# A third buffer for raw weights in the first of two layers, paid for with smaller pools of statistics

## The chip, the cores and the metric

The kernel runs on one core of a Trainium2 chip. The metric is the device time of one execution in microseconds (us). In the profile PE is TensorE's matrix multiplies, PEld its weight loads, DVE is VectorE, ACT is ScalarE, POOL is GpSimd, and SP is the queue from which this kernel issues all of its DMAs.

## What is computed

A decoder trunk of two layers on 512 positions of width 1024, in float32. The core of the reference:

```python
def even_layer(x, ...):               # layer 0
    q, k, v, g_ret, xb, g_lru = split(x @ w_in)          # six parts of 1024 columns
    ret = retention(rope(q), rope(k) * dk**-0.5, v)      # 8 heads, decay per head
    ret = groupnorm(ret) * gn_g + gn_b
    ret = ret * silu(g_ret)
    lru = rg_lru_branch(xb, ...) * silu(g_lru)           # conv of width 4, gates, scan
    return concat([ret, lru]) @ w_out

def odd_layer(x, ...):                # layer 1
    q, k, v, g = split(x @ w_in)                         # four parts of 2048 columns
    out = diff_attention(rope(q) * dh**-0.5, rope(k), v, lam)   # 8 heads, two softmax maps each
    out = rmsnorm(out) * subln_g * (1 - lambda_init) * silu(g)
    return out @ w_out

h = layer_norm(alpha * h + layer(h))  # after each layer
```

## The kernel before

**Number format.** Matrix products are made from float32 in two parts. `split` (L140) writes a high part with ACT (a cast, L146) and a low part with DVE (a subtraction, L147). `mm3` (L149) then issues three matmuls: high by high (L150) and the two cross products (L151, L152). Each weight passes through this as well.

**Weights.** There are 144 weight tiles of 128 x 1024 (512 KB each), named w0, w1 and so on in the order of their use. Tiles w0 to w63 belong to the first layer. `fetch` (L164) takes the next one. It allocates a raw tile from the pool `wraw` (two buffers), issues its DMA from SP (L172), and splits it into a pair from the pool `wsp` (five pairs). In the profile `w_r` is a raw tile, `w19h` and `w19l` are the parts of weight 19. A raw buffer is free again when its cast and its subtraction are done. A pair is free when the last matmul with that weight is done. `take` (L179) calls `fetch` until the weight in use and up to two more have been written into the program.

**Order.** PE and SP run in the order in which the program is written (`manual_schedule`, L118). ACT, DVE and POOL are ordered by the framework when the kernel is built, by priorities (`high_priority`) and by when it reckons an instruction to be ready. On the chip each engine runs its own queue in order and waits on semaphores.

**The first layer** runs a list of units, `ev` (L249): products of one weight with the whole input (`t_unit`: gates `gl` and `gr`, `xb`, `q`, `k`), value projections `v` in two halves of four weights (`s_unit`), and output products (`out_unit`). Between the matmuls of a unit `side.tick()` (L190) lets the heads' own work in: `retention` (L432) and `lru` (L475) are generators that are resumed after set numbers of ticks. `retention` makes four score products (`rs`), multiplies them with a decay table on DVE (`rsd`, L440), splits them (`r`), sums them with the values (`ro`), squares and averages the result (`rq`, `rv`), and normalizes it. `lru` makes a convolution (`xc`), two gates (`pr`, `pi`) and a scan. Both use the pool `es` of temporaries. The decay tables (`dec`, two buffers in the pool `two`) and the parameters of the first layer norm (`ln`) are also loaded from SP (L156). The pools `es`, `qkp` and `two` belong to the first layer and close with it (`phase`, L368 and L589).

**Statistics.** The pool `small` has four buffers a tag. In it are the means of the value projection (`vm`, L418), the two halves' sums of a layer norm (`bst`), their mean and variance (`bmv`), the reciprocal deviation (`lrs`) and, in one block of the last norm, `lnm`. A layer norm handles four blocks of 128 positions.

Of the kernel before, what the change touches and what calls it, by code (L numbers as in the profile page):

```python
# [8 lines left out]
F32 = mybir.dt.float32  # L9
# [5 lines left out]
P = 128  # L15
D = 1024
# [80 lines left out]
def trunk(ctx: ExitStack, tc: tile.TileContext, a):  # L97
# [3 lines left out]
    def pool(name, bufs, stack=ctx, **kw):  # L101
        return stack.enter_context(tc.tile_pool(name=name, bufs=bufs, **kw))

    const = pool("const", 1)
    big = pool("big", 1)
    wraw = pool("wraw", 2)
    wsp = pool("wsp", 5)
    vp = pool("vp", 4)
    mixp = pool("mixp", 3)
# [3 lines left out]
    small = pool("small", 4)  # L113
# [8 lines left out]
    def work(name):  # L122
        return wk.tile([P, S], F32, tag="wk", name=name)
# [4 lines left out]
    def bank(pl, tag, name):  # L128
        return pl.tile([P, 512], F32, tag=tag, name=name)

    def pair(pl, shape, tag, name, **kw):
        return tuple(pl.tile(shape, F32R, tag=tag + x, name=name + x, **kw) for x in "hl")
# [4 lines left out]
    def cut(t, *ix):  # L137
        return t[0][ix], t[1][ix]

    def split(src, dst, scale=None):  # L140
        if scale is not None:
            s = sg[:, scale:scale + 1]
            nc.scalar.activation(out=dst[0], in_=src, func=AF.Identity, scale=s)
            nc.vector.scalar_tensor_tensor(out=dst[1], in0=src, scalar=s, in1=dst[0].bitcast(F32), op0=ALU.mult, op1=ALU.subtract)
            return
        nc.scalar.copy(out=dst[0], in_=src)  # L146
        nc.vector.tensor_tensor(out=dst[1], in0=src, in1=dst[0].bitcast(F32), op=ALU.subtract)  # L147

    def mm3(out, l, r, start, stop):  # L149
        nc.tensor.matmul(out=out, lhsT=l[0], rhs=r[0], start=start, stop=False)  # L150
        nc.tensor.matmul(out=out, lhsT=l[0], rhs=r[1], start=False, stop=False)  # L151
        nc.tensor.matmul(out=out, lhsT=l[1], rhs=r[0], start=False, stop=stop)  # L152

    def load(name, shape, src, pl=None, tag=None, bufs=None):
        t = (pl or const).tile(shape, F32, tag=tag or name, name=name, bufs=bufs)
        nc.sync.dma_start(out=t, in_=src)  # L156
        return t
# [6 lines left out]
    def fetch(parts=((0, D),)):  # L164
        if len(ready) < len(order):
            n = len(ready)
            src, scale = order[n]
            raw = wraw.tile([P, D], F32, tag="raw", name=f"w{n}_r")
            w = pair(extra.pop(n, wsp), [P, D], "w", f"w{n}")
            for lo, hi in parts:  # L170
                c = slice(lo, hi)
                nc.sync.dma_start(out=raw[:, c], in_=src[:, c])  # L172
                split(raw[:, c], cut(w, ALL, c), scale=scale)
                yield
            ready.append(w)
# [3 lines left out]
    def take(ahead):  # L179
        taken[0] += 1  # L180
        while len(ready) < min(taken[0] + ahead, len(order)):
            list(fetch())
        return ready[taken[0] - 1]
# [36 lines left out]
    def out_unit(mix, y, name, first, before=None, after=None, late=0):  # L220
        n = len(mix)
        w = [take(1 if n == 2 else 0) for _ in range(n)]
        for sb in range(SB):
            pss = [bank(ps_pj, "pj", f"{name}_ps{sb}{hf}") for hf in range(2)]
            steps = [(c, hf) for c in range(0, n, 2) for hf in range(2)]
            if late and sb == SB - 1:
                steps.sort(key=lambda t: t[1])
            for c, hf in steps:
                if before is not None and hf == 0:
                    before(c // 2, sb)  # L230
                for i in range(c, c + 2):
                    mm3(pss[hf], cut(mix[i], ALL, slice(sb * P, sb * P + P)), cut(w[i], ALL, slice(hf * HALF, hf * HALF + HALF)), i == 0, i == n - 1)
                    side.tick()
            for hf, ps in enumerate(pss):
                yy = y[:, sb, hf * HALF:hf * HALF + HALF]
                with tc.high_priority(late):
                    if first:
                        nc.vector.scalar_tensor_tensor(out=yy, in0=yy, scalar=ALPHA, in1=ps, op0=ALU.mult, op1=ALU.add)
                    else:
                        nc.vector.tensor_tensor(out=yy, in0=ps, in1=yy, op=ALU.add)  # L240
                    if late:
                        if hf == 0:
                            st = small.tile([P, 2, 6], F32, tag="bst", name="bst")
                        nc.vector.bn_stats(out=st[:, hf], in_=yy)
                        stats[sb] = st
            if after is not None:
                after(sb)
# [9 lines left out]
    for kind, i in ev:  # L257
        if kind in ("ro", "lo", "out"):
            order += [(eo[2 * i + j + n], None) for n in {"ro": (0,), "lo": (8,), "out": (8, 0)}[kind] for j in range(2)]
        else:  # L260
            n = 4 if kind == "v" else 1
# [67 lines left out]
    def layer_norm(y, sb, gb, late=None):  # L329
        hv = [y[:, sb, hf * HALF:hf * HALF + HALF] for hf in range(2)]  # L330
        st = stats.pop(sb, None)
        if st is None:
            st = small.tile([P, 2, 6], F32, tag="bst", name="bst")
            for hf in range(2):
                nc.vector.bn_stats(out=st[:, hf], in_=hv[hf])
        mv = small.tile([P, 2], F32, tag="bmv", name="bmv")
        nc.vector.bn_aggr(out=mv, in_=st)  # L337
        rs = small.tile([P, 1], F32, tag="lrs", name="lrs")
        if late is not None:
            ve = small.tile([P, 1], F32, tag="rs", name="lve")  # L340
            nc.vector.tensor_scalar(out=ve, in0=mv[:, 1:2], scalar1=EPS, scalar2=None, op0=ALU.add)
            nc.gpsimd.tensor_tensor(out=rs, in0=ve, in1=nhalf[:, :1], op=ALU.pow)
        else:
            rsqrt(mv[:, 1:2], rs, 1.0, EPS)
        if late:

            nm = small.tile([P, 1], F32, tag="lnm", name="lnm")
            nc.gpsimd.tensor_scalar(out=nm, in0=mv[:, 0:1], scalar1=rs, scalar2=-1.0, op0=ALU.mult, op1=ALU.mult)
            nc.scalar.activation(out=hv[1], in_=hv[1], func=AF.Identity, scale=rs, bias=nm)
            nc.gpsimd.tensor_tensor(out=hv[1], in0=hv[1], in1=gb[0][1], op=ALU.mult)  # L350
            nc.gpsimd.tensor_tensor(out=hv[1], in0=hv[1], in1=gb[1][1], op=ALU.add)
            nc.vector.scalar_tensor_tensor(out=hv[0], in0=hv[0], scalar=mv[:, 0:1], in1=gb[0][0], op0=ALU.subtract, op1=ALU.mult)
            nc.vector.scalar_tensor_tensor(out=hv[0], in0=hv[0], scalar=rs, in1=gb[1][0], op0=ALU.mult, op1=ALU.add)
            yield from enumerate(hv)
            return
        for hf in range(2):
            nc.vector.scalar_tensor_tensor(out=hv[hf], in0=hv[hf], scalar=mv[:, 0:1], in1=gb[0][hf], op0=ALU.subtract, op1=ALU.mult)
        for hf in range(2):
            nc.vector.scalar_tensor_tensor(out=hv[hf], in0=hv[hf], scalar=rs, in1=gb[1][hf], op0=ALU.mult, op1=ALU.add)
            yield hf, hv[hf]  # L360
# [7 lines left out]
    phase = ctx.enter_context(ExitStack())  # L368
    es = pool("es", 10, phase)
    qkp = pool("qkp", 2, phase)  # L370
    two = pool("two", 2, phase)
    y = big.tile([P, SB, D], F32, tag="y", name="y")
    vecs = load("vecs", [P, 8, KT], a["vecs"])
    conv_w = lambda i, c: vecs[:, i, c:c + 1]
# [37 lines left out]
    def v_even(i):  # L412
        out = []

        def evac(sb, ps):
            with tc.high_priority(P_VALUE):
                p3 = ps.rearrange("p (h e) -> p h e", e=P)
                m = small.tile([P, 4], F32, tag="vm", name="vm")  # L418
                nc.vector.tensor_reduce(out=m, in_=p3, axis=AX.X, op=ALU.add)
                nc.vector.tensor_scalar(out=m, in0=m, scalar1=1.0 / P, scalar2=None, op0=ALU.mult)  # L420
                c = work("vc")
                nc.vector.tensor_tensor(out=c.rearrange("p (h e) -> p h e", e=P), in0=p3, in1=m.unsqueeze(2).broadcast_to([P, 4, P]), op=ALU.subtract)
                t = pair(vp, [P, S], "v", f"ev{i}{sb}")
                split(c, t)
            out.append(t)

        s_unit(x, f"ev{i}", i == 1, evac, lambda sb: None)
        return out
# [89 lines left out]
    m, job, seen = {}, {}, set()  # L518
# [15 lines left out]
    for kind, i in ev:  # L534
# [5 lines left out]
        elif kind == "xb":  # L540
            if i % 2 == 0:
                raw = load(f"gw{i}", [P, 4 * P], a["gw"][i // 2], pl=es, tag="es")
# [44 lines left out]


    phase.close()  # L589
    lq = load("lq", [P, 4, P], a["lq"].partition_broadcast(P), pl=wk, tag="wk")  # L590
    nc.vector.tensor_tensor(out=lq[:, 0:2], in0=lq[:, 0:2], in1=lq[:, 2:4], op=ALU.mult)
    ls = const.tile([P, 2], F32, tag="ls", name="ls")
# [199 lines left out]
```

## Time and profile before

| | |
|---|---|
| median of three runs | 940.38 us (940.04 to 940.52) |
| the profiled execution | 940.23 us, of which 938.4 us from the first to the last instruction |
| PE busy | 922.6 us, 98% |
| PEld busy | 764.8 us, 82% |
| DVE busy | 693.8 us, 74% |
| ACT busy | 462.8 us, 49% |
| POOL busy | 59.2 us, 6% |
| granted TensorE clock, mean | 0.998 |
| DMA | 88.94 MB, mean 95 GB/s |
| loads of first-layer weights | 63 of 512 KB and one in two halves |

Two things help in reading the rows. Matmuls overlap, and the end of a matmul is modelled. Its row is longer than the distance to the next one, so lost time is seen in the starts. And a wait at the end of a row, `[1.57 <-DMA w_r<-in_ev_w]`, is idle time of that engine before the instruction, with what ended it.

### The profile page before, as it was taken

What the parts mean: (1) busy time and instruction counts of PE and PEld (TensorE: products, weight loads), DVE (VectorE), ACT (ScalarE), POOL (GpSimd) and SP (SyncE); (2) the same over time, 40 slices, a digit from 0 to 9 for tenths busy, and PEclk for the clock granted to TensorE, in tenths of its full rate; (3) what the DMA queues carried; (4) which work ended last, traced back from release to release, by engine and by line L of the source; (5) the groups of instructions that cost most, each with busy time, mean ns of one, the idle gap of its engine ahead of it and who ended that gap; (6) DMA issues with size and microseconds to landing.
All of it is one profiled execution on the core that took longest, in us unless ns stands there. A gap on an engine that the chain in (4) does not pass through costs nothing.

```text
span 938.4 us, 11555 instructions
## 1 busy us (share of the span) xinstructions
PE 922.6 (98%) x4327; PEld 764.8 (82%) x4327; DVE 693.8 (74%) x1171; ACT 462.8 (49%) x750; POOL 59.2 (6%) x118
## 2 busy tenths in 40 slices
PE   9999999999999999999999999999999999999996
PEld 7888888878888788888887888888888888888885
DVE  5877997867869988994489864578754488637677
ACT  5567786566384776423334455233453234444230
POOL 0000000000000000000001210100100101101023
PEclk9999999999999999999999999999999999999999
DMA  6562221512414123304222222132222141223102
GB/s 225 168 222 71 79 80 56 169 57 70 144 34 168 57 90 115 124 23 168 90 91 68 68 83 76 45 126 98 68 68 90 45 135 68 69 89 113 67 23 90
DMA packets 27417, 88.94 MB, mean 95 GB/s; under 512 B 3425, under 2 KB 3553, under 8 KB 27361
## 3 DMA queue, kind: packets, MB, share of 16 engines
q1 hardware_dynamic: 27360, 88.20, 28.3%
q8 instruction: 34, 0.56, 0.3%
q14 instruction: 23, 0.18, 0.1%
HBM read 86.09 MB, written 2.10 MB: 94 GB/s over the span
## 4 chain that ended last, share of the span: by engine, by line
PE 68%; DVE 16%; ACT 7%; issue 3%; DMA 3%; POOL 2%; SPq 0%; DVEq 0%; POOLq 0%; ACTq 0%
PE ov_ps L152 3%; PE ov_ps L151 3%; PE ov_ps L150 3%; PE og_ps L150 3%; PE og_ps L151 3%; PE og_ps L152 3%; PE oo_ps L150 3%; PE oo_ps L151 2%; PE oo_ps L152 2%; DMA w_r<-in_ev_w 2%; PE xb_ps L151 1%; PE xb_ps L150 1%; PE out_ps L150 1%; PE xb_ps L152 1%; PE out_ps L152 1%
## 5 line engine op out<-in xcount | busy, mean ns | idle before, releaser
L611 ACT ACTIVATE e<-as,nm 128x128 f32<-128x128 f32 (+3 forms) x64 | 33.1, 523 | 26.5 <-DVE nm L608 26.3
L642 DVE SCALAR_TENSOR_TENSOR o<-po,ars,og 128x256 f32<-128x256 f32 x32 | 15.5, 484 | 36.0 <-POOL ars L327 36.0
L608 DVE CUSTOM_DVE_ANT_0 as<-as,mask 128x128 f32<-128x128 f32 (+3 forms) x64 | 30.3, 510 | 1.9 <-PE as L152 1.9
L618 POOL TENSOR_SCALAR zr<-z 128x1 f32<-128x1 f32 x32 | 11.2, 351 | 316.3 <-ACT e L611 316.3
L326 POOL TENSOR_SCALAR rs_t<-bmv 128x1 f32<-128x1 f32 x6 | 2.2, 375 | 419.7 <-DVE bmv L337 419.7
L638 ACT ACTIVATE po<-po 128x256 f32<-128x256 f32 x32 | 11.9, 372 | 25.2 <-PE po L152 25.0
L326 POOL TENSOR_SCALAR rs_t<-ss,zr 128x1 f32<-128x1 f32 x32 | 16.0, 502 | 129.2 <-ACT po L638 123.8
L327 POOL TENSOR_TENSOR ars<-rs_t,nhalf 128x1 f32<-128x1 f32 x32 | 20.4, 638 | 2.7
L240 DVE TENSOR_TENSOR y<-oo_ps,y 128x512 f32<-128x512 f32 x24 | 16.4, 685 | 4.2 <-PE oo_ps L152 4.2
L483 DVE SCALAR_TENSOR_TENSOR xc<-xbp,vecs,xc 128x509 f32<-128x509 f32 (+2 forms) x24 | 17.9, 746 | 1.4 <-ACT xc L480 1.2
L619 DVE SCALAR_TENSOR_TENSOR e<-e,zr,e 128x128 f32<-128x128 f32 (+3 forms) x32 | 17.6, 551 | 1.0
L616 DVE RECIPROCAL zr<-z 128x1 f32<-128x1 f32 x32 | 5.2, 163 | 14.9 <-ACT e L611 14.7
L440 DVE TENSOR_TENSOR rsd<-rs,dec 128x512 f32<-128x512 f32 (+3 forms) x32 | 15.5, 486 | 1.0 <-PE rs L152 0.9
L646 PEld LDWEIGHTS po<-ident,o 128*128 128x128 f32 x64 | 8.3, 140 | 7.7 <-DVE o L642 4.8
L623 PE MATMUL wt<-ident,e 128*128 128x128 f32 x80 | 14.0, 272 | 0.0
L646 PE MATMUL po<-ident,o 128*128 128x128 f32 x64 | 12.6, 277 | 1.4 <-DVE o L642 1.2
L623 PEld LDWEIGHTS wt<-ident,e 128*128 128x128 f32 x80 | 10.5, 140 | 3.9 <-DVE e L619 0.4
L146 ACT CAST hh<-ht 128x512 fp32r<-128x512 f32 x8 | 4.7, 589 | 18.1 <-PE ht L578 18.1
L499 DVE TENSOR_TENSOR xbp<-xbp,xc 128x512 f32<-128x512 f32 x8 | 5.5, 692 | 9.8 <-ACT xbp L496 9.8
L611 ACT ACTIVATION_READ_ACCUMULATOR e<-as,nm 128x1 f32 x64 | 12.6, 196 | 0.0
L505 DVE SCALAR_TENSOR_TENSOR xc<-t,r 128x512 f32<-128x512 f32 x8 | 5.5, 690 | 9.0 <-ACT r L504 9.0
L409 ACT ACT_TABLE_LOAD x9 | 11.5, 1283 | 0.6 <-PE gl_ps L152 0.4
(2673 smaller groups left out, 3414.7 us busy)
## 6 DMA issues: line engine op xcount, KB each, us to landing
w_r<-in_od_w SPq DMA_DIRECT2D x64, 512.0 KB, 3.3
w_r<-in_ev_w SPq DMA_DIRECT2D x47, 512.0 KB, 3.3
w_r<-in_ev_wo SPq DMA_DIRECT2D x16, 512.0 KB, 3.3
w_r<-in_od_wo SPq DMA_DIRECT2D x16, 512.0 KB, 3.3
dec<-in_dec SPq DMA_DIRECT2D x8, 256.0 KB, 3.7
y<-in_x SPq DMA_DIRECT2D x4, 512.0 KB, 6.8
out_h<-y SPq DMA_DIRECT2D x8, 256.0 KB, 2.0
xr<-in_xt SPq DMA_DIRECT2D x3, 512.0 KB, 6.9
```

Of the source, the lines that this page charges most:

```text
L150: nc.tensor.matmul(out=out, lhsT=l[0], rhs=r[0], start=start, stop=False)
L151: nc.tensor.matmul(out=out, lhsT=l[0], rhs=r[1], start=False, stop=False)
L152: nc.tensor.matmul(out=out, lhsT=l[1], rhs=r[0], start=False, stop=stop)
L240: nc.vector.tensor_tensor(out=yy, in0=ps, in1=yy, op=ALU.add)
L326: nc.gpsimd.tensor_scalar(out=t, in0=var, scalar1=scale, scalar2=eps, op0=ALU.mult, op1=ALU.add)
L327: nc.gpsimd.tensor_tensor(out=out, in0=t, in1=nhalf[:, :1], op=ALU.pow)
L483: nc.vector.scalar_tensor_tensor(out=xc[:, sh:], in0=xb[:, :S - sh], scalar=conv_w(w, c), in1=xc[:, sh:], op0=ALU.mult, op1=ALU.add)
L608: nc.vector.tensor_tensor_reduce(out=ps[:, :n], in0=ps[:, :n], in1=mask[:, S - n:], scale=-QK_SCALE, scalar=3.0e38, op0=ALU.add, op1=ALU.m ...
L611: nc.scalar.activation(out=e, in_=ps[:, :n], func=AF.Exp, scale=-1.0, bias=nm, accum_out=z[:, mp:mp + 1])
L619: nc.vector.scalar_tensor_tensor(out=ee[0], in0=ee[1], scalar=zr[:, 0:1], in1=ee[0], op0=ALU.mult, op1=ALU.add)
L623: nc.tensor.transpose(out=pt[:, kb * P:kb * P + P], in_=ee[0][:, kb * P:kb * P + P], identity=ident)
L646: nc.tensor.transpose(out=pm[:, i * P:i * P + P], in_=o[:, i * P:i * P + P], identity=ident)
```

## The change

The raw weights of the first layer get a third buffer, of 4 KB a partition. It is a pool of its own, `wraw3`, that opens with the first layer's other pools and closes with them. `wraw` becomes a list: two entries of the old pool before and after, and a third entry, the new pool, in between. `fetch` takes the entry n modulo the length of the list. The first three weights are fetched before the third entry exists. Where four buffers of `bst`, `bmv`, `lrs` and `vm` were kept, there are two, and one of `lnm`.

```diff
-    wraw = pool("wraw", 2)
+    wraw = [pool("wraw", 2)] * 2
...
-            raw = wraw.tile([P, D], F32, tag="raw", name=f"w{n}_r")
+            raw = wraw[n % len(wraw)].tile([P, D], F32, tag="raw", name=f"w{n}_r")
...
-                            st = small.tile([P, 2, 6], F32, tag="bst", name="bst")
+                            st = small.tile([P, 2, 6], F32, tag="bst", name="bst", bufs=2)
...
-            st = small.tile([P, 2, 6], F32, tag="bst", name="bst")
+            st = small.tile([P, 2, 6], F32, tag="bst", name="bst", bufs=2)
...
-        mv = small.tile([P, 2], F32, tag="bmv", name="bmv")
+        mv = small.tile([P, 2], F32, tag="bmv", name="bmv", bufs=2)
...
-        rs = small.tile([P, 1], F32, tag="lrs", name="lrs")
+        rs = small.tile([P, 1], F32, tag="lrs", name="lrs", bufs=2)
...
-            nm = small.tile([P, 1], F32, tag="lnm", name="lnm")
+            nm = small.tile([P, 1], F32, tag="lnm", name="lnm", bufs=1)
...
     two = pool("two", 2, phase)
+    wraw.append(pool("wraw3", 1, phase))
...
-                m = small.tile([P, 4], F32, tag="vm", name="vm")
+                m = small.tile([P, 4], F32, tag="vm", name="vm", bufs=2)
...
     phase.close()
+    wraw.pop()
```

## The prediction

> **What bounds the kernel now.** I read the page's busy table first, then the busy time by stage, then the waits of the tensor engine in the first layer, and then the rows around each of them. The change reaches the first layer alone, so the stage that counts is 24 to 390 us. The columns of the second view are PE, PEld, DVE, ACT and POOL busy, granted clock, DMA share and GB/s.
>
> ```profile
> span 938.4 us, 11555 instructions
> PE 922.6 (98%) x4327; PEld 764.8 (82%) x4327; DVE 693.8 (74%) x1171; ACT 462.8 (49%) x750; POOL 59.2 (6%) x118
> ```
>
> ```profile
> 24.00:390.00 366.00, 362.99 (x1644) 300.71 (x1643) 303.84 (x451) 238.57 (x313) 0.00 (x0) 1.00 0.32 105
> ```
>
> PE is the bound: it lacks 366.00 - 362.99 = 3.01 us of being busy all through the stage, at a granted clock of 1.00. DVE, at 303.84 / 366 = 83%, is next. The idle time understates the stalls, because matmuls overlap. In a stretch without waits, from the first of the rows below to the second, 14 steps take 3.17 us, or 0.226 us each, while each row is drawn 0.39 us long. A wait shows only after 0.39 - 0.23 = 0.16 us of it has been covered. What is lost at a place is therefore the distance from start to start less 0.23.
>
> ```profile
> 296.53 0.39 PE L150 MATMUL q_ps<-xh,w47h 128*128 128x512 f32 x1
> 299.70 0.39 PE L152 MATMUL q_ps<-xh,w47l 128*128 128x512 f32 x1
> ```
>
> The waits of PE from 10 to 390 us (two more are shown as timeline rows further down):
>
> ```profile
> PE rv L457 <- ACT rq7h L146: 0.5, 1, 0.5
> PE ro L151 <- DVE r31l L147: 0.5, 1, 0.5
> PE ev_ps L151 <- DVE w3l L147: 0.3, 1, 0.3
> PE rs L150 <- DVE rsd L440: 0.3, 1, 0.3
> PE rv L458 <- DVE rq7l L147: 0.2, 1, 0.2
> PE ro L151 <- DVE r53l L147: 0.2, 1, 0.2
> ```
>
> Only one of them, w3l, is a weight that comes late, and w3 keeps its old buffer and its old wait (below). The others are steps of a head's chain (scores, squares, gates) that come late out of the DVE or ACT queue. So a third raw buffer can only help by an indirect way. A cast of a weight that waits for its DMA holds up ACT, and whatever stands behind it on ACT and DVE.
>
> That does happen. Idle time before the casts and splits of raw weights, by what ended it (the view of the tile w_r, 0 to 390 us):
>
> ```profile
>   DMA w_r<-in_ev_w: 27.4, 16
>   DMA w_r<-in_ev_wo: 13.9, 6
> ```
>
> ACT stands 41.3 us in 22 waits. Most of that costs PE nothing, since ACT is busy only 238.57 of the 366 us.
>
> **The change part by part.** *The rotation.* The first five weights, w0 to w4, come from the old pool of two with the same waits as before; w5 is the first in the new buffer, then every third. From w5 on the load of weight n waits for the split of n-3 at the latest, instead of n-2. The place where a PE wait lies nearest to such a load:
>
> ```profile
> 78.59 1.23 DVE L147 TENSOR_TENSOR w16l<-w_r,w16h 128x1024 fp32r<-128x1024 f32 x1 [0.43 <-ACT w16h L146]
> 102.69 1.22 DVE L147 TENSOR_TENSOR w17l<-w_r,w17h 128x1024 fp32r<-128x1024 f32 x1
> 103.94 2.66 SPq L172 DMA_DIRECT2D w_r<-in_ev_w  x2
> 107.34 1.05 ACT L146 CAST w19h<-w_r 128x1024 fp32r<-128x1024 f32 x1 [1.57 <-DMA w_r<-in_ev_w]
> 108.43 1.23 DVE L147 TENSOR_TENSOR w19l<-w_r,w19h 128x1024 fp32r<-128x1024 f32 x1 [0.51 <-ACT w19h L146]
> 113.80 0.39 PE L150 MATMUL pr<-xc2h,gw2h 128*128 128x512 f32 x1
> 114.26 0.50 PE L151 MATMUL pr<-xc2l,gw2h 128*128 128x512 f32 x1
> 114.12 1.22 DVE L147 TENSOR_TENSOR w20l<-w_r,w20h 128x1024 fp32r<-128x1024 f32 x1
> ```
>
> The load of w19 is issued at 103.94, 0.03 us after the split of w17 ended (102.69 + 1.22). With three buffers it follows the split of w16, which ended at 79.82, so it has landed long before ACT reaches the cast. ACT's 1.57 us and DVE's 0.51 us go. The gate matmul at 114.26 comes 0.46 us after its forerunner instead of 0.23. What is late there is xc2l, which DVE makes just ahead of w20l. DVE 0.51 us earlier covers the 0.23: **-0.2 us**, between 0 and -0.23. Late next would be the square of the same head, just below.
>
> ```profile
> 122.28 0.60 ACT L146 CAST rq1h<-rq 128x512 fp32r<-128x512 f32 x1
> 122.93 0.51 PE L457 MATMUL rv<-rq1h,ones 128*128 128x512 f32 x1
> 123.66 0.50 PE L458 MATMUL rv<-rq1l,ones 128*128 128x512 f32 x1 [0.22 <-DVE rq1l L147]
> ```
>
> The second rv matmul starts 0.73 us after the first, a loss of 0.50. Its input is released by ACT's cast rq1h, which has no idle time before it: ACT's queue decides. Bounds 0 and -0.50. I take **-0.2**, nearer to nothing, because the wait that goes lies 15 us earlier in that queue.
>
> ```profile
> ACT w49h L146 <- DMA w_r<-in_ev_wo: 3.1, 1, 3.1
> ```
>
> ```profile
> 302.42 0.39 PE L152 MATMUL q_ps<-xh,w47l 128*128 128x512 f32 x1
> 303.35 0.68 DVE L308 TENSOR_TENSOR q_c<-q_ps,cos 128x512 f32<-128x512 f32 x1
> 305.01 0.40 PE L152 MATMUL pr<-xc6h,gw6l 128*128 128x512 f32 x1
> 305.47 0.56 DVE L440 TENSOR_TENSOR rsd<-rs,dec 128x384 f32<-128x384 f32 x1
> 306.08 0.50 PE L150 MATMUL pi<-xc6h,gw6h 128*128 128x512 f32 x1 [0.67 <-DVE rsd L440]
> ```
>
> Here PE loses 306.08 - 305.01 - 0.23 = 0.84 us. The bank for pi is freed by a product on DVE (rsd) that stands behind a rope begun at 303.35. DVE is behind by then, and the 3.1 us for which ACT stood before the cast of w49 lie some 15 us earlier. If DVE comes out ahead, the rope still cannot begin before its matmuls end at 302.42 + 0.39 = 302.81. So at most 0.54 us can be had: bounds 0 and -0.54, and I take the middle, **-0.3**.
>
> ```profile
> 357.21 10.46 SPq L156 DMA_DIRECT2D ln<-in_ev_ln  x4
> 366.28 1.22 DVE L147 TENSOR_TENSOR w59l<-w_r,w59h 128x1024 fp32r<-128x1024 f32 x1
> 367.78 7.79 SPq L172 DMA_DIRECT2D w_r<-in_ev_wo  x3
> 372.91 1.05 ACT L146 CAST w61h<-w_r 128x1024 fp32r<-128x1024 f32 x1 [5.71 <-DMA w_r<-in_ev_wo]
> ```
>
> The largest pair of PE waits, rq7h and rq7l (0.5 and 0.2 us drawn, some 1.1 with the covered parts), lies behind the cast of w61, which waits 5.71 us. But this load stands in SP's queue behind four loads of norm parameters, the last of which is issued at 357.21 + 10.46 = 367.67, waiting for slots that the third raw buffer does not free. The split of w59 ended at 367.50, so taking that condition away gains at most 0.1 us. **0**, between -1.1 (ACT's order changes) and 0. The same holds for loads that SP has queued behind a decay table, for which it waits 26.0 us in all:
>
> ```profile
> SPq L156 <- DVE rsd L440: 26.0, 3, 16.2
> ```
>
> Nothing is gained at r31l, rsd and r53l: their chains wait for no raw weight. Other casts are held by the split buffers, five pairs, which stay:
>
> ```profile
> 191.67 1.05 ACT L146 CAST w34h<-w_r 128x1024 fp32r<-128x1024 f32 x1 [0.51 <-PE xb_ps L151]
> ```
>
> *Order on ACT and DVE.* The framework orders these two when the kernel is built, by priority and estimated readiness. Raw weights that are ready sooner can be split sooner, also ahead of a head's chain. One split is 1.22 us on DVE (the w20l row). At a place with slack it costs nothing. At the waits above it costs up to 1.22, or gains as much by being out of the way. I put the net at **0**, with -1.2 and +2.4 (one split out of the way, two in it) for the range.
>
> *Statistics tiles.* Two instead of four. The sums of the value projection (vm) and the norm's bn tiles are written by DVE and, but for one short read of bmv by POOL, read by DVE, which runs them one after another. What crosses engines goes at the pace of the norm's blocks; lrs stands for it:
>
> ```profile
> 398.28 1.41 DVE L359 SCALAR_TENSOR_TENSOR y<-y,lrs,ln 128x512 f32<-128x512 f32 x2
> 410.65 0.55 POOL L327 TENSOR_TENSOR lrs<-rs_t,nhalf 128x1 f32<-128x1 f32 x1
> ```
>
> The third block's lrs is written at 410.65, and the first block's was last read at 399.69: 11 us apart, so **0**. lnm is made once in the whole kernel. With two vm tiles the fourth block's reduce has to follow the second block's subtraction, and DVE has them in that order already: **0**:
>
> ```profile
> 31.36 0.68 DVE L422 TENSOR_TENSOR vc<-ev_ps,vm 128x512 f32<-128x512 f32 x1
> 32.02 0.68 DVE L419 TENSOR_REDUCE vm<-ev_ps 128x4 f32<-128x512 f32 x1
> ```
>
> The pool for the third buffer closes with the layer, after which the loads run as before. The second layer keeps its time.
>
> *Sum.* -0.2 - 0.2 - 0.3 + 0 + 0 = -0.7 us. The profiled execution took 940.23 us (1.8 outside the span) against a median of 940.38. So 940.23 - 0.7 = **939.5 us**, 0.1% below the median.
>
> **The rivals.** *Every PE wait that a DMA wait has a part in goes* (faster). The sum at its bounds: 0.23 + 0.50 + 0.84 + 1.1 = 2.7, and with the small gap that follows each wait some 3.1: 937.1 us. For it: ACT's 41.3 us of standing is large beside 3 us. Against it: two of the four are bound by SP's queue and by a rope.
>
> *Nothing moves*: the loads come earlier, but SP's other loads, the split buffers or DVE decide, and PE's waits stay: 940.2. The w34h and ln rows speak for it, the w19 row against it.
>
> *Splits get in the way* (slower). Around 114 us DVE has no hole between 108.43 and the matmul that waits. If the splits of w20 and w21, ready earlier, are put ahead of xc2l, PE waits 2 x 1.22 = 2.4 us there: 942.7. One split, 1.22, is less than can be measured; from two on a PE chain it decides. For it: w20's load will follow the split of w17 instead of w18, so it is ready a few us sooner in a full stretch. Against it: DVE also drops the idle time it had.
>
> *PE has far more to give than the waits show.* A measure by weight loads gives this: they are busy 300.71 of 366 us, and 65 us would be open. Against it are the matmul rows at 0.226 us apiece with no wait between them, in the same stage; no buffer shortens that. [...] I give it 1 in 100, at some 930 us.
>
> **How the numbers follow.** About 0.2%, 1.9 us, is what a measurement of this kernel can tell from no change. The forecast (938.6 to 940.0) has 0.38, nothing moves 0.22, the faster rival 0.23 with the last one's 0.01, the slower one 0.16. The faster and slower cases count fully outside 0.2%, the other two inside: 0.24 faster, 0.60 same, 0.16 slower. The range runs from just under the faster rival, 936.9, to 942.2, short of the slower one's 942.7; about 0.15 lies outside.
>
> **What would show it.** Right: no ACT wait for DMA at w19h and far under 41 us in the stage; loads issued 0.03 us after the split of n-3; the pr wait gone; w61h still waiting some 5 us; PE idle from 24 to 390 us between 2.2 and 3.0. Wrong: the rq7 waits gone (faster), or new PE waits over 1 us behind a DVE split (slower), or a changed second layer, which I have priced at nothing.

## The result, and the profile after

The changed kernel takes 942.88 us (median; 942.32 to 944.65) against 940.04 for the kernel before in the same comparison: 1.0030 times as long, 95% interval 1.0021 to 1.0040. It is 2.8 us slower, where 0.7 us less than the profiled execution of before was forecast.

First the span, the busy table and the busy time by stage after (columns as before), then the idle time before the casts and splits of raw weights up to 390 us:

```profile
span 942.9 us, 11557 instructions
PE 926.5 (98%) x4327; PEld 766.2 (81%) x4327; DVE 693.6 (74%) x1171; ACT 461.8 (49%) x750; POOL 59.9 (6%) x118
24.00:390.00 366.00, 362.42 (x1628) 298.92 (x1627) 300.55 (x446) 234.94 (x311) 0.00 (x0) 1.00 0.30 103
390.00:925.00 535.00, 532.70 (x2585) 443.02 (x2584) 364.93 (x661) 213.16 (x421) 53.16 (x106) 1.00 0.25 82
```

```profile
  DMA w_r<-in_ev_w: 17.7, 10
  DMA w_r<-in_ev_wo: 6.9, 1
```

The third buffer did what it does: ACT's waits for raw weights fell from 41.3 us in 22 places to 24.6 in 11. PE gained nothing from that: in the 366 us it is busy 0.57 us less than before. The waits of PE from 10 to 390 us show one large new figure, for head 7's split (0.5 before):

```profile
PE rv L458 <- ACT rq7h L146: 1.4, 1, 1.4
PE ro L151 <- DVE r31l L147: 0.5, 1, 0.5
PE pi L150 <- DVE rsd L441: 0.4, 1, 0.4
PE pr L151 <- DVE xc2l L147: 0.2, 1, 0.2
```

I paired the 4,327 matmuls of two profiled executions in order and compared the distances from start to start. The profiled execution after took 944.65 us, 1.8 above the median, because of something that the second one does not show (last section), so the account is made with the second profiled execution of the same kernel, e1_after below: span 941.0, against 938.4 before. The 2.62 us between them:

| where | us |
|---|---|
| distances below 0.3 us in both, all over the kernel | +1.81 |
| the gate matmuls at 114 us | +0.59 |
| head 7's squares at 375 us | +0.56 |
| pi behind the rope at 306 us | -0.25 |
| all else | -0.09 |

Each row compares one execution with one. The executions below that keep two raw buffers and the old order of loads differ from this one of before as well, by -0.13 to -0.34 us at 114 us, by -0.21 to +0.37 at 306 us and by -0.02 to -0.26 at 375 us (e2, e9, e10, e16). So the second and the third row are clear of that, and the fourth is not.

The first row is no wait at all. In what follows it is called the spacing. By this account two thirds of the loss is matmuls that follow each other a little more slowly, in the second layer too, where no instruction or buffer count of theirs differs. A stretch of 85 steps without a wait, its first and last matmul, in before and then in after:

```profile
410.06 0.39 PE L150 MATMUL ov_ps<-w64h,hh 128*128 128x512 f32 x1
427.60 0.39 PE L150 MATMUL ov_ps<-w64h,hh 128*128 128x512 f32 x1
```

```profile
414.12 0.40 PE L150 MATMUL ov_ps<-w64h,hh 128*128 128x512 f32 x1
431.86 0.40 PE L150 MATMUL ov_ps<-w64h,hh 128*128 128x512 f32 x1
```

It took 17.54 us before and 17.74 after, and it takes one of these two, to 0.01 us, in every kernel below but one.

The gate at 114 us, first two rows of DVE before (the split of w20 follows them at 114.12), then after. The rows after are SP (the loads of w19 and w20), then ACT, DVE and PE:

```profile
112.03 0.74 DVE L483 SCALAR_TENSOR_TENSOR xc<-xbp,vecs,xc 128x511 f32<-128x511 f32 x1
113.51 0.69 DVE L147 TENSOR_TENSOR xc2l<-xc,xc2h 128x512 fp32r<-128x512 f32 x1
```

```profile
81.73 22.77 SPq L172 DMA_DIRECT2D w_r<-in_ev_w  x2
103.22 1.05 ACT L146 CAST w19h<-w_r 128x1024 fp32r<-128x1024 f32 x1
107.51 1.05 ACT L146 CAST w20h<-w_r 128x1024 fp32r<-128x1024 f32 x1 [1.51 <-DMA w_r<-in_ev_w]
111.17 0.74 DVE L484 SCALAR_TENSOR_TENSOR xc<-xbp,vecs,xc 128x510 f32<-128x510 f32 x1
111.83 1.22 DVE L147 TENSOR_TENSOR w20l<-w_r,w20h 128x1024 fp32r<-128x1024 f32 x1
112.97 0.75 DVE L484 SCALAR_TENSOR_TENSOR xc<-xbp,vecs,xc 128x511 f32<-128x511 f32 x1
114.48 0.50 PE L150 MATMUL pr<-xc2h,gw2h 128*128 128x512 f32 x1
115.20 0.50 PE L151 MATMUL pr<-xc2l,gw2h 128*128 128x512 f32 x1 [0.23 <-DVE xc2l L147]
```

ACT's wait before w19h is gone, as forecast, and a wait of 1.51 us before w20h has taken its place. On DVE the split of w20 stands between two steps of the convolution that makes xc, where before it stood behind xc2l. It costs the first gate matmul some 0.3 us and the second another 0.26.

The layer's end, after: the loads of w61, w62, w63 are issued within 2.65 us where before it took them 7.79, and the load of lq, parameters of the second layer, follows at once.

```profile
369.07 2.65 SPq L172 DMA_DIRECT2D w_r<-in_ev_wo  x3
371.78 0.52 SPq L156 DMA_DIRECT2D lq<-in_lq  x1
375.39 1.05 ACT L146 CAST w61h<-w_r 128x1024 fp32r<-128x1024 f32 x1 [6.89 <-DMA w_r<-in_ev_wo]
376.97 0.62 ACT L146 CAST rq7h<-rq 128x512 fp32r<-128x512 f32 x1
377.64 0.49 PE L458 MATMUL rv<-rq7h,ones 128*128 128x512 f32 x1 [1.40 <-ACT rq7h L146]
378.37 0.54 PE L459 MATMUL rv<-rq7l,ones 128*128 128x512 f32 x1 [0.23 <-DVE rq7l L147]
```

ACT reaches the cast of w61 and stands there for 6.89 us (5.71 before), with head 7's work queued behind it. The cast begins 6.32 us after the load was issued (369.07 to 375.39); before it was 5.13 (367.78 to 372.91). The DMA rows for 366 to 377 us, before and then after, have the three weights' median from issue to landing as the last number:

```profile
w_r<-in_ev_wo SPq DMA_DIRECT2D x3, 512.0 KB, 4.1
```

```profile
w_r<-in_ev_wo SPq DMA_DIRECT2D x3, 512.0 KB, 6.5
```

### The profile page after: what moved, and what is told of

The parts are those of the page before. It is cut to its first block, busy times and chain, and to the rows that moved or that the text cites. A ratio compares the mean times of both kernels' runs of the same rounds, so it can differ in the third digit from the quotient of the medians.

```text
span 942.9 us, 11557 instructions
## 1 busy us (share of the span) xinstructions
PE 926.5 (98%) x4327; PEld 766.2 (81%) x4327; DVE 693.6 (74%) x1171; ACT 461.8 (49%) x750; POOL 59.9 (6%) x118
## 4 chain that ended last, share of the span: by engine, by line
PE 68%; DVE 17%; ACT 7%; issue 4%; DMA 2%; POOL 2%; SPq 0%; DVEq 0%; POOLq 0%; ACTq 0%
PE ov_ps L152 3%; PE ov_ps L151 3%; PE ov_ps L150 3%; PE og_ps L150 3%; PE og_ps L151 3%; PE og_ps L152 3%; PE oo_ps L150 2%; PE oo_ps L152 2%; PE oo_ps L151 2%; PE ev_ps L151 1%; PE ev_ps L152 1%; PE ev_ps L150 1%; DMA w_r<-in_ev_w 1%; PE out_ps L150 1%; PE out_ps L152 1%
```

## The experiments

Three theories stood at the start. S: at the layer's end the loads that may now go sooner share the DMA engines with w61 and make it late. O: the order at 114 us. D: the slower spacing of matmuls. All ratios are against the kernel before, timed on the same chip beside each group of runs: 939.97 us for e1 to e5, 939.94 for e6 and e9 to e11, 939.81 for e13 to e16. Runs of different groups are compared by what they lie above it.

**The change again (e1_after).** No edit.

> The changed kernel once more, unedited, for a second profile. Theory S (shared DMA engines at the end of the layer): w61 again lands 6 us or more after its issue because w62 and w63 are issued within 2.5 us of it, the first rv matmul of head 7 again waits 1.5 us or more, and the drop of the granted clock behind it is not in every execution, since six of seven times lie at 942.3 to 943.0 and the profiled one at 944.65. Theory D (drift): the matmul spacing in the first layer is again about 1 ns longer than before, which would be 1.5 us over the layer. Theory O (order): the pr wait at 114 us is again some 0.5 us longer than before, because the split of w20 stands inside the convolution. Time 942.3 to 943.0.

942.75 us, 1.0028 (1.0018 to 1.0038); the account above is its. The spacing was again 1.8 us slower, so D is no accident of one execution.

**The statistics tiles alone (e2_stats).** The third pool is never opened.

```
-    wraw.append(pool("wraw3", 1, phase))
...
-    wraw.pop()
```

> Only the smaller pools of statistics tiles; the raw pool has two buffers as before. All of S, O and D: the time before, 940.0 with at most 0.5 either way, since nothing of PE's waits hangs on these tiles. The rival, that two vm tiles reorder DVE during the first value projection and that this costs: 940.6 or more, with new PE waits between 25 and 60 us.

941.33 us, 1.0013 (1.0005 to 1.0022): half the loss, from the part I had priced at nothing. It shows no wait: the pairs of matmuls above 0.3 us apart gain 1.45 us in sum (0.62 of it at the start of the kernel, where executions differ), and the spacing loses 1.76. What the reductions do besides is to move tiles. The pool of the small tiles shrinks by 416 bytes of a partition, and every pool opened behind it (es, q and k, gate weights, decays, the second layer's extra weights) starts at byte 180096 where it was 180512. That gave theory P, placement: where the tiles lie counts, not their number.

**The third buffer given back ahead of w61 (e4_end2).**

```
+    wraw.pop()
     ident = load("ident", [P, P], a["ident"])
...
     phase.close()
-    wraw.pop()
```

> The changed kernel, with the third buffer given up just before w61 is fetched; the order of every engine's instructions is that of the changed kernel. Theory S: w62 and w63 are held back again until the splits of w60 and w61 are done, w61 lands after about 5 us, the first rv wait of head 7 falls from 1.5 to about 0.65 us, the clock keeps at 1.00 there: 941.3 to 941.8, 1 us or more under the changed kernel of the same call. Theories O and D: unchanged, 942.3 to 943.0.

941.94 us, 1.0019 (1.0011 to 1.0028), 0.8 below the change: a little less of a gain than S gave, and just outside its range, but below that of O and D. The loads are spread again, and w61 is cast 1.3 us sooner than in the profiled execution after, 5.05 us after its issue where it was 6.32:

```profile
369.06 7.72 SPq L172 DMA_DIRECT2D w_r<-in_ev_wo  x3
374.11 1.05 ACT L146 CAST w61h<-w_r 128x1024 fp32r<-128x1024 f32 x1 [5.62 <-DMA w_r<-in_ev_wo]
376.36 0.50 PE L458 MATMUL rv<-rq7h,ones 128*128 128x512 f32 x1
```

The order of instructions is the change's on every engine; only the time at which w62 and w63 may be issued differs. So w61 is late because these two follow it sooner. That they slow it by sharing the DMA engines is the reading of it; no run looks into the engines.

**w61 loaded ahead of the identity and the norm parameters, three buffers (e5_w61).**

```
+    list(fetch())
     ident = load("ident", [P, P], a["ident"])
```

> The changed kernel with one more fetch ahead of the loads of the identity and of the norm parameters, so that SP issues the load of w61 before them. Theory S: ACT no longer stands before the cast of w61, all waits of rv of head 7 go (1.5 + 0.5 + 0.1 us) and the clock keeps: 940.2 to 940.9. Theories O and D: the loss lies elsewhere, and at most the 0.65 + 0.5 us that stood there before the change can be had besides: 941.2 or more.

940.84 us, 1.0008 (0.9999 to 1.0016): 1.9 below the change, at the upper end of what S gave. The whole loss of PE at 375 us is gone, also the part that before has (-1.25 us against before there). What is left above before is the spacing, 1.75, and the gate at 114 us, 0.57.

**The same edit with two buffers (e6_w61_two).** The kernel before with that one line.

> The kernel before (two raw buffers, four statistics tiles) with the load of weight tile 61 issued ahead of the loads of the identity and the norm parameters at the end of the first layer. In before it is issued at 367.78 us and lands 5.11 us later, and head 7's split waits behind its split on ScalarE. Theory S (the loads that share the DMA engines with w61 at the layer's end set when it lands): alone on the queue it is issued at about 367.5 and lands in 3.3 to 3.9 us, before head 7's product is there, the PE wait of 0.5 us for head 7's split goes, and so does the one of 0.2 behind it; 939.0 to 939.6 us. If the wait there has another cause (the split of head 7 itself): 939.8 to 940.2.

941.19 us, 1.0013 (1.0004 to 1.0022): slower, a miss. At 375 us PE gains the 1.25 as in e5, but then loses 2.03 at 387 to 390:

```profile
368.59 1.85 SPq L156 DMA_DIRECT2D ln<-in_ev_ln  x4
376.84 1.05 ACT L146 CAST w62h<-w_r 128x1024 fp32r<-128x1024 f32 x1 [2.73 <-DMA w_r<-in_ev_wo]
388.64 1.22 DVE L147 TENSOR_TENSOR w63l<-w_r,w63h 128x1024 fp32r<-128x1024 f32 x1
389.92 0.50 PE L151 MATMUL eo_ps<-w63l,retm3h 128*128 128x512 f32 x1 [0.59 <-DVE w63l L147]
```

The load of w62 now follows close behind the norm parameters, as that of w61 did before, and its cast is the one that waits. The weights behind it come late in turn. One wait was traded for another; in e5, with three buffers, nothing is lost at 387 to 390 us.

**The tiles put back (e9_pad416).** The statistics reductions with an unused tile behind them.

```
     small = pool("small", 4)
+    pad = pool("pad", 1).tile([P, 104], F32, tag="pad", name="pad")
```

> The statistics reductions alone, with an unused tile of 416 bytes of a partition behind the pool of the small tiles. The reductions made that pool 416 bytes smaller, so every pool opened behind it (the work tiles es, q and k, gate weights, decays; in the second layer the extra weights and q, k) moved from byte 180512 to 180096; the tile moves them back. Theory P (placement): the cost of the reductions alone (941.33 against 939.97 us, with 1.76 us more in the sum of the matmuls' spacings below 300 ns) is where those tiles lie, not their number. Then the sum of spacings is within 0.3 us of before's, and the time 939.7 to 940.3. Theory B (fewer buffers, or the other order of the start that they bring): the spacings stay 1.5 us or more above before's and the time is 941.0 to 941.7.

940.04 us, 0.9999 (0.9991 to 1.0008); spacing 0.05 us below before's. The reductions themselves cost nothing that this run can tell.

**The kernel before, moved by 96 bytes (e10_b96).** The same line with 24 elements, added to before.

> The kernel before with nothing but an unused tile of 96 bytes of a partition behind the pool of the small tiles: all pools behind it start at byte 180608, which is 512 bytes above where the changed kernel has them, and 96 above before. No instruction, wait or buffer count differs. Theory P, if what counts is the place within a step of 512 bytes or a part of it: the sum of the matmul spacings rises by 1.4 to 1.9 us as in the reductions alone, and the time is 941.0 to 941.7. Theory B: nothing changes, 939.7 to 940.3. A third outcome, no rise here but a return in the run with 416 bytes, would mean that placement counts but by another step.

941.14 us, 1.0012 (1.0004 to 1.0021); spacing +1.87 us. An unused tile alone brings the loss: every engine has the same instructions as in before, in the same order. The stretch of 85 steps in e9_pad416 (17.54 us) and in e10_b96 (17.74):

```profile
409.85 0.39 PE L151 MATMUL ov_ps<-w64h,hh 128*128 128x512 f32 x1
427.39 0.39 PE L151 MATMUL ov_ps<-w64h,hh 128*128 128x512 f32 x1
```

```profile
411.41 0.40 PE L151 MATMUL ov_ps<-w64h,hh 128*128 128x512 f32 x1
429.15 0.40 PE L151 MATMUL ov_ps<-w64h,hh 128*128 128x512 f32 x1
```

**The change, moved by 32 bytes (e11_a32).** The same line with 8 elements, added to the change.

> The changed kernel with an unused tile of 32 bytes behind the pool of the small tiles: the pools behind it start at byte 180128, which has the place of before's 180512 within a step of 64 or 128 bytes (32), though not within one of 256 or 512. More does not fit beside the third raw buffer. If placement counts within 64 or 128 bytes, the sum of the matmul spacings falls back by 1.4 to 1.9 us and the time is 940.9 to 941.5 (942.75 for the change less 1.4 to 1.8; the wait for head 7's split at 375 us stays 1 us or more). If it counts by a larger step, or buffer counts are the cause, the time stays at 942.4 to 943.0.

942.39 us, 1.0026 (1.0016 to 1.0037). The spacing is 1.18 us above before's, between the two, and the stretch is the exception, 17.67. So the place within 64 or 128 bytes doesn't decide alone.

**All large tiles moved by 96 bytes (e16_all96).** In before:

```
     const = pool("const", 1)
+    pad = const.tile([P, 24], F32, tag="pad", name="pad")
```

> The kernel before with an unused tile of 96 bytes ahead of all the large tiles, so that every one of them moves by 96 bytes, those ahead of the small ones too, and lies to each other as in before. Theory P with the place relative to the other tiles: nothing changes, spacings within 0.3 us of before's and 939.7 to 940.3 us. With the place itself: all matmuls read moved tiles, and the spacings rise by at least the 1.8 us of the run in which only the pools behind the small tiles had moved by 96: 941.2 us or more (or fall, if for the tiles ahead this place is the better one: a change of more than 1 us either way).

939.56 us, 0.9997 (0.9988 to 1.0006); spacing 0.19 below before's. So what counts, as far as this one move shows, is where the tiles lie to each other.

**The change with before's placement (e13_place).** Three small tiles of the second layer (zr, ss, ars) in three buffers, which moves the pools behind them to 180000, exactly 512 below before's place. One of the three edits:

```
-            ss = small.tile([P, 1], F32, tag="ss", name="ss")
+            ss = small.tile([P, 1], F32, tag="ss", name="ss", bufs=3)
```

> The whole change, with three of the second layer's small tiles in three buffers where they had four (96 bytes less), so that the pools behind them start at byte 180000: 512 below before's 180512, where the change has 180096. No instruction is moved. Theory P (the place within 512 bytes): the sum of the matmul spacings falls from 1.8 us above before's to within 0.3 of it, and the time from 942.75 to 941.0 to 941.6; what is left against before is the wait for head 7's split at 375 us and the later gate product at 114 us. If the two raises of 1.2 us measured so far were something else of those kernels, it stays at 942.4 to 943.0.

941.66 us, 1.0023 (1.0014 to 1.0032): 1.85 above before, where the change had 2.78, so 0.9 less. It is just above the stated range, with the spacing 0.08 below before's. The losses at 114 us (0.71) and 375 us (1.12) are still there and are as large as the rest.

**Placement and early w61 together (e14_place_w61)**, the line of e5 added:

> The whole change with the same 96 bytes less and with weight tile 61 loaded ahead of the identity and the norm parameters at the layer's end. Theories P and S together: no PE wait for head 7's split, spacings as before, 939.0 to 939.7 us, below before (939.95). If the two causes don't add: 940.2 or more.

939.44 us, 0.9995 (0.9986 to 1.0004), not to be told from before. The causes add: the early w61 took 1.91 us off in e5 and takes 2.22 off here. The gate at 114 us is then the one loss left, 0.88 us in this execution:

```profile
112.31 1.22 DVE L147 TENSOR_TENSOR w20l<-w_r,w20h 128x1024 fp32r<-128x1024 f32 x1
113.44 0.74 DVE L484 SCALAR_TENSOR_TENSOR xc<-xbp,vecs,xc 128x511 f32<-128x511 f32 x1
114.94 0.51 PE L150 MATMUL pr<-xc2h,gw2h 128*128 128x512 f32 x1 [0.46 <-ACT xc2h L146]
```

**The third buffer from weight 24 on (e15_late)**, otherwise as e14:

```
-            raw = wraw[n % len(wraw)].tile([P, D], F32, tag="raw", name=f"w{n}_r")
+            raw = wraw[n % len(wraw) if n >= 24 else 0].tile([P, D], F32, tag="raw", name=f"w{n}_r")
```

> As the run before, with the third raw buffer used from weight tile 24 on alone, so that tiles 5 to 23 are loaded and split as with two buffers. Theory O (the split of tile 20 ahead of the gate convolution on VectorE makes the gate product at 114 us 0.5 to 0.6 us later): this loss goes, the early waits of PE stay as before, 938.6 to 939.3 us, and the offset of PE against before is below 0.3 us at 116 us where the run before has 0.6. If the third buffer costs nothing there, it is as the run before.

938.91 us, 0.9990 (0.9981 to 0.9998), 0.5 below e14 as theory O gave, and the fastest of all: 0.9 us below before. The split of w20 stands behind xc2l again, the gate matmuls run without a wait, and so do head 7's squares:

```profile
112.96 0.69 DVE L147 TENSOR_TENSOR xc2l<-xc,xc2h 128x512 fp32r<-128x512 f32 x1
113.57 1.22 DVE L147 TENSOR_TENSOR w20l<-w_r,w20h 128x1024 fp32r<-128x1024 f32 x1
113.50 0.39 PE L150 MATMUL pr<-xc2h,gw2h 128*128 128x512 f32 x1
374.09 0.39 PE L458 MATMUL rv<-rq7h,ones 128*128 128x512 f32 x1
374.32 0.39 PE L459 MATMUL rv<-rq7l,ones 128*128 128x512 f32 x1
```

## Why the prediction was wrong

*What bounds the kernel, and how the buffer works*: right. PE bounds it, a weight that comes late is not what PE waits for, and w19 behaved as said. ACT's waits fell by 16.7 us, and the most that PE can have had of it is the 0.25 at pi.

*Statistics tiles, 0*: the term that failed most, 0.9 to 1.4 us of the 2.8 by the medians of e2, e10 and e13. The spacing in the profiles is 1.8. Part of it seems to come back where PE would wait anyway: at 375 us e2 and e10 lose 0.26 less than before, and e9 and e16, with before's spacing, 0.05 and 0.02 less. The working about who reads which tile when was right: with the places restored the reductions cost nothing (e9). What was left out is that a smaller pool moves all that is allocated behind it. "The second layer keeps its time" was wrong for the same reason, in spacing, not in waits.

*w61, 0, between -1.1 and 0*: the sign was wrong. It cost 0.56 us in e1_after, 1.12 in e13, and in the profiled execution after, whose wait was 1.40 us against 0.5, about 0.9; holding back w62 and w63 (e4) gave back 0.8. The condition was read correctly (w61's own issue comes no sooner), but I asked only when w61 may be issued, not what may be issued right behind it. The step "late next" was not applied to the queue itself: w62, w63 and lq are now issued within 2.7 us behind it, and it lands over a microsecond later (e4).

*w19 and pr, -0.2*: +0.59. The gain on ACT was real but went to the next weight. The mechanism that I gave to the slower rival came true at the place it named, with one split and not two in front of the chain (e15 against e14: 0.5 us). Its 942.7 us is near the measured time by a sum of other things. The order on ACT and DVE, put at a net 0, is this same item; elsewhere its changes cost nothing that the traces show.

*pi, -0.3*: -0.25, near in number. That the third buffer brought it is not shown: e2, with two buffers, has -0.21 there, and e10 +0.37, though all kernels with three have -0.16 to -0.27. *rq1h, -0.2*: nothing; the wait removed 15 us ahead of it was replaced at once.

The bounds did not hold the two waits that grew: pr (0 to -0.23) came to +0.59, w61 (0 to -1.1) to +0.56. By medians the three causes are 0.9 to 1.4 us (places), 0.8 (w61, e4) and 0.5 (order, e15 against e14), 2.2 to 2.7 of the 2.8. Without the places the time would have lain inside the range (e13, 941.66), but still above before and not below it. The places were in no row of the trace that I priced.

## What to carry to other kernels

A change in the size of any small pool is a change in the place of every tile behind it: run it once with an unused tile that restores the places, before any wait is made responsible. When a buffer lets loads go sooner, look at which load a queue of work already waits for, and at what will then be in flight beside it. A gain in an engine's waits is worth what the next instruction in its queue can do with it: here 16.7 us on ACT bought at most 0.25 on PE.

## What the runs showed of the hardware

In this kernel the distance between matmuls depends on where tiles lie to each other. With the later pools at byte 180512 (before, e9), or 512 below (e13), or with all large tiles moved alike (e16), the 85 steps take 17.54 us; moved by +96 (e10) or -416 bytes (after) they take 17.74, by -384 bytes (e11) 17.67. Some 350 of 2,800 single 512-wide matmuls go from 226 or 227 ns to mostly between 230 and 237, also ones whose own two operands have not moved, while whole stretches (150 to 180 and 210 to 240 us) don't change. In e1_after and e10_b96 13% of these matmuls are over 3 ns slower where DVE, ACT or POOL has an instruction within 0.1 us of them, and 16 of 278 where none has. That accesses of other engines slow them would fit the most of that, but not the 16, and no run shows it; what slows the matmuls stays open, and so does whether 512 bytes is the step.

In the stream of matmuls the granted clock fell in one of the fourteen profiled executions, behind head 7's wait. The mean granted clock is 0.996 in it and 0.997 or 0.998 in the other thirteen. (At the end it falls as well: in before 4.83 us after the last matmul, in the profiled execution after 4.18.) Columns as above, the clock being the third number from the end; the profiled execution after, then e1_after with nearly the same wait:

```profile
376.00:379.00 3.00, 1.37 (x5) 0.77 (x4) 2.27 (x3) 2.97 (x5) 0.00 (x0) 0.95 0.52 168
379.00:382.00 3.00, 3.00 (x8) 2.32 (x8) 3.00 (x5) 2.95 (x4) 0.00 (x0) 0.50 0.38 153
```

```profile
376.00:379.00 3.00, 1.73 (x7) 1.03 (x6) 2.61 (x3) 2.95 (x6) 0.00 (x0) 1.00 0.56 188
379.00:382.00 3.00, 3.00 (x14) 2.46 (x14) 3.00 (x6) 2.96 (x3) 0.00 (x0) 1.00 0.31 124
```

At 0.50 only 8 matmuls began in 3 us, where e1_after has 14: from start to start it is 0.43 us instead of 0.23. This and a wait longer by 0.35 us at the head make up what that execution lies above the median. The clock was at 0.50 for 3.41 us, from 378.69 us on, and at 1.00 for 368.64 us ahead of that and 556.37 us behind it. In before it was at 1.00 for 925.01 us without a break. These three are 108, 163 and 271 times the 3.413 us of the trace, each to within 0.1 us; two traces show that, and no cause of it. In the last 3.41 us ahead of the fall at the end PE is without work in both. But in the 3.41 us ahead of the fall behind head 7's wait, PE was without work for only 1.63 us, in two pieces (1.40 and 0.23). In e13_place PE waits there for 1.6 and 0.2 us, and the clock's mean, 0.998, leaves no room for such a fall, which takes 0.0018 off it, beside the one at the end. So why the clock fell in this one execution stays open.
